# A residual stored before its affine part, and modulation steps spread anew

## The chip, the cores and the metric

The kernel is one program on one core of a Trainium2 chip. The metric is the device time of one execution in microseconds (us). Everything is fp32; TensorE (PE) multiplies each fp32 operand as a high and a low half, so one product of two fp32 tiles is three matrix instructions. VectorE (DVE) and ScalarE (ACT) prepare those halves, SyncE (SP) issues nearly all transfers from one queue, in order, and GpSimd (POOL) does little.

## The reference, cut to what matters

A two-layer backbone works on 512 latent tokens and 256 context tokens of width 1024. Each layer has a half-step SwiGLU feed-forward, a mixer (layer 0: a bidirectional HGRN2 recurrence, layer 1: a chunked spatial-gating MLP), and a second feed-forward. Each of these is wrapped in the same way:

```python
def modulate(x, m, k):
    return x * (1 + m[..., 3 * k + 1, :]) + m[..., 3 * k, :]

def post_norm_update(x, y, m, k, g, b):
    return layer_norm(DN_ALPHA * x + m[..., 3 * k + 2, :] * y, g, b)

def macaron_half_ffn(x, m, k, w_in, w_out, g, b):
    return post_norm_update(x, 0.5 * swiglu(modulate(x, m, k), w_in, w_out), m, k, g, b)

def chunk_mlp(h, n_chunks, w_in, v_g, v_b, w_s, b_s, w_out):
    u, v = jnp.split(jax.nn.gelu(h @ w_in), 2, axis=-1)
    v = layer_norm(v, v_g, v_b)
    v = v.reshape(bsz, n_chunks, CM_CHUNK, CM_GROUPS, CM_INNER // CM_GROUPS)
    v = jnp.einsum('gts,bnsgc->bntgc', w_s, v) + b_s.T[None, None, :, :, None]
    return (u * v.reshape(bsz, length, CM_INNER)) @ w_out

    mx = modulation(c, mod_w[i], mod_b[i])     # silu(c) @ mod_w + mod_b: nine rows of 1024
    x = macaron_half_ffn(x, mx, 0, ...)        # ffn (i, 0), context too where it is needed
    x = post_norm_update(x, mixer(modulate(x, mx, 1)), mx, 1, ...)
    x = macaron_half_ffn(x, mx, 2, ...)        # ffn (i, 1)
```

The residual that goes from one wrapped sub-layer to the next is the layer norm's result, g * z + b, where z is the row less its mean and divided by its deviation. The next sub-layer reads it twice: modulated, as the operand of its first product, and times alpha in its own sum before the norm.

## The kernel before

**Stages.** In order of time: ffn (0,0) of the latent, then of the context (`FeedContext`); the HGRN heads; ffn (0,1); ffn (1,0); the chunk MLP, first its value half (8 groups of 4 token tiles), then its gating half (8 groups `gi` of 3 column tiles `ci`), then its output product; ffn (1,1). A weight tile of 512 KB comes by one transfer into `raw` (3 buffers), is split into its halves by ACT (L136) and DVE (L137), and stands in `w` (6 buffers); this is `unit`, L140.

**A feed-forward** has an up half and a down half. The up half after the first two feature tiles is `FeedSums.rest`: for each of 22 tiles f it loads a gate tile `raw` and an up tile `rawu` and replaces eight block products by seven. DVE makes the sums of weights for it (L572 to L576, on `e`, `rawu`, `raw`) and splits four tiles; PE then does seven products of twelve matrix instructions into `psc`, `pse` and `psa`. The down half is `OutPhase`. `lead` and `part` multiply the hidden tiles `hs` with the weights into `y`; `evac` adds `y` to the residual tile `x` and gathers statistics; `norm` makes z in place (L329); `operand` transposes z on PE into `pt` (L339) and applies norm affine and modulation in one step (L349, L351) to give `xm`.

**The transition** is what stands between the last `y` of one sub-layer and the steady loop of the next. In it PE does transposes and, as `xm` comes in, the first products `psf` of the next sub-layer (`staged`); DVE does `evac`, `norm`, `operand`, and then `FeedSums.sums` (L532), which builds the token sums `f4` to `f7` for the seven products. Right behind these, the residual is stored: `store` (L288 to L299) loads g and b as rows (`rg`, `rb`), makes alpha * (g * z + b) in 16 DVE instructions (L296, L297, 128x512 each) and sends 8 transfers of 256 KB to `x2`, `x3`, `x4` or `x5`. The next `OutPhase` loads those tiles back and adds `y` without more ado (`scaled` is True).

**The modulation rows** come from 18 products of a vector with a 1024x1024 matrix, which DVE does beside the other work. One task of `mod_task` is one such matrix: eight steps, each with a 512 KB transfer into `mraw` (2 buffers) and two DVE instructions per condition (L171, `junk`). `mod_step(n)` takes n steps off the queue; calls stand in the loops of the latent ffn (0,0), of the context (one step per feature tile and per pair of hidden tiles), of the HGRN heads (2 and 5 per head from head 1 on) and of the value half of the chunk MLP (one per token tile). `made` drains the queue up to a row that is needed now.

**The order of the work.** Each engine works its list in order. The list is made by a scheduler that moves instructions within what data and buffers permit; `issue_after` holds an instruction behind another.

## Time and profile before

| | before |
|---|---|
| time, median of 3 runs (lowest to highest) | 2534.65 us (2533.74 to 2537.7) |
| the profiled execution's own time | 2532.92 us |
| its span, from the first to the last instruction | 2531.2 us |
| mean granted TensorE clock in it | 0.992 |
| PE busy, share of the span | 2449.0 us, 97% |
| DVE busy, share of the span | 1882.1 us, 74% |
| ACT busy, share of the span | 1100.1 us, 43% |
| transfers | 368.06 MB, mean 145 GB/s |

The span is 1.7 us shorter than that execution's time, and the median of the runs is another 1.7 us longer. PE is busy nearly all the time, so what counts is where it is not, and where it ran at a lower clock. The stages, on the time axis of the profile: latent ffn (0,0) to about 395 us, the context to 590 us, HGRN heads 680 to 1010 us, ffn (0,1) to 1377 us, ffn (1,0) to 1740 us, value half to 1876 us, gating half to 2020 us, its output product to 2163 us, ffn (1,1) to the end. The transitions are at 1010 to 1067, 1377 to 1418, 1732 to 1762 and 2163 to 2212 us.

### The profile page before, as it was taken

To read this page: it belongs to the slowest core of one execution; us is meant where nothing else is said; L and a number is where in the kernel's file an instruction comes from. 1 tells how busy PE (TensorE), PEld (TensorE's weight loads), DVE (VectorE), ACT (ScalarE), POOL (GpSimd) and SP (SyncE) were. 2 spreads that over 40 slices of the span, in tenths; PEclk is the share of its full clock that TensorE was granted. 3 is DMA by queue.
4 is the path that set the end of the run, shared out by engine and by line. 5 is a ranking of instruction groups with operands and counts; after the bars stand their busy time and mean duration, and the time that the engine had idled before them with its cause. 6 is when DMAs were issued, how large, how long until landed. Compare 5 with 4: busy or idle time off the path is not lost.

```text
span 2531.2 us, 37425 instructions
## 1 busy us (share of the span) xinstructions
PE 2449.0 (97%) x14687; PEld 2199.0 (87%) x14687; DVE 1882.1 (74%) x3361; ACT 1100.1 (43%) x1671; POOL 49.3 (2%) x82
## 2 busy tenths in 40 slices
PE   7999999999999899899999999999999999899998
PEld 5888889978888788899988999988998888899987
DVE  7965479784599986988756988657787345988765
ACT  4222434453444452455643555533332233455641
POOL 0000000000000000000000000000010000000001
PEclk9999999999999999999999999999999999999999
DMA  8866357974234414333332433324963223333332
GB/s 320 290 200 198 104 171 237 313 251 132 69 123 134 142 59 142 121 117 101 126 112 71 167 103 114 110 96 156 312 202 109 83 92 114 114 114 109 109 101 79
DMA packets 111170, 368.06 MB, mean 145 GB/s; under 512 B 12760, under 2 KB 16016, under 8 KB 110992
## 3 DMA queue, kind: packets, MB, share of 16 engines
q1 hardware_dynamic: 110992, 365.65, 43.5%
q8 instruction: 115, 1.88, 0.3%
q14 instruction: 63, 0.52, 0.1%
HBM read 352.99 MB, written 12.61 MB: 144 GB/s over the span
## 4 chain that ended last, share of the span: by engine, by line
PE 69%; DVE 17%; DMA 7%; ACT 3%; issue 2%; POOL 1%; SPq 0%; POOLq 0%; DVEq 0%; ACTq 0%
PE y L151 7%; PE y L149 7%; PE y L150 7%; PE psc L149 4%; PE psc L151 4%; PE psc L150 4%; PE psf L150 4%; PE psf L151 3%; PE psf L149 3%; DVE junk L171 2%; PE pse L149 2%; DVE w L137 2%; PE pse L151 2%; PE pse L150 2%; DMA raw<-in_ffn_w_in 2%
## 5 line engine op out<-in xcount | busy, mean ns | idle before, releaser
L137 DVE TENSOR_TENSOR w<-raw,w 128x1024 fp32r<-128x1024 f32 (+1 forms) x458 | 516.0, 1131 | 181.8 <-ACT w L136 179.6
L136 ACT ACTIVATE w<-raw 128x1024 fp32r<-128x1024 f32 (+1 forms) x458 | 449.7, 984 | 405.7 <-PE y L151 91.2
L149 PE MATMUL y<-w,hs 128*128 128x512 f32 x984 | 384.5, 391 | 4.4 <-ACT hs L136 4.4
L151 PE MATMUL y<-w,hs 128*128 128x512 f32 x984 | 384.6, 391 | 2.3 <-DVE hs L137 2.3
L150 PE MATMUL y<-w,hs 128*128 128x512 f32 x984 | 383.5, 390 | 0.0
L137 DVE TENSOR_TENSOR hs<-h,hs 128x512 fp32r<-128x512 f32 (+1 forms) x220 | 136.1, 635 | 151.0 <-ACT hs L136 151.0
L136 ACT ACTIVATE hs<-h 128x512 fp32r<-128x512 f32 (+1 forms) x220 | 126.2, 587 | 241.1 <-PE y L151 230.9
L151 PEld LDWEIGHTS y<-w,hs 128*128 128x128 f32 x984 | 185.1, 188 | 44.7 <-DVE hs L137 6.1
L149 PEld LDWEIGHTS y<-w,hs 128*128 128x128 f32 x984 | 185.2, 188 | 44.5 <-ACT hs L136 6.6
L150 PEld LDWEIGHTS y<-w,hs 128*128 128x128 f32 x984 | 185.1, 188 | 38.0
L149 PE MATMUL psf<-xm,w 128*128 128x512 f32 (+1 forms) x544 | 192.0, 361 | 19.0 <-ACT xm L136 18.6
L151 PE MATMUL psf<-xm,w 128*128 128x512 f32 (+1 forms) x544 | 193.8, 357 | 1.5 <-DVE w L137 1.5
L150 PE MATMUL psf<-xm,w 128*128 128x512 f32 (+1 forms) x544 | 194.5, 359 | 0.5 <-DVE xm L137 0.5
L171 DVE SCALAR_TENSOR_TENSOR junk<-mraw,srow_x 128x512 bf16<-128x512 f32 x256 | 165.7, 684 | 13.9 <-DMA mraw<-in_mod_w 13.9
L149 PE MATMUL pse<-f,w 128*128 128x256 f32 x480 | 137.2, 286 | 6.9 <-ACT silu L483 6.9
L151 PE MATMUL psc<-xm,w 128*128 128x256 f32 x480 | 136.2, 284 | 4.0 <-DVE w L137 4.0
L150 PE MATMUL pse<-f,w 128*128 128x256 f32 x480 | 136.9, 285 | 0.0
L151 PE MATMUL pse<-f,w 128*128 128x256 f32 x480 | 136.9, 285 | 0.0
L149 PE MATMUL psc<-f,w 128*128 128x256 f32 x480 | 136.5, 284 | 0.0
L150 PE MATMUL psc<-f,w 128*128 128x256 f32 x480 | 136.2, 284 | 0.0
L151 PE MATMUL psc<-f,w 128*128 128x256 f32 x480 | 136.1, 284 | 0.0
L149 PE MATMUL psc<-xm,w 128*128 128x256 f32 x480 | 135.8, 283 | 0.0
(258 smaller groups left out, 5913.2 us busy)
## 6 DMA issues: line engine op xcount, KB each, us to landing
raw<-in_ffn_w_in SPq DMA_DIRECT2D x160, 512.0 KB, 4.5
mraw<-in_mod_w SPq DMA_DIRECT2D x144, 512.0 KB, 4.6
raw<-in_ffn_w_out SPq DMA_DIRECT2D x110, 512.0 KB, 3.6
rawu<-in_ffn_w_in SPq DMA_DIRECT2D x60, 512.0 KB, 3.5
raw<-in_hg_wf SPq DMA_DIRECT2D x32, 512.0 KB, 4.3
raw<-in_cm_wv SPq DMA_DIRECT2D x32, 384.0 KB, 4.5
raw<-in_cm_wu SPq DMA_DIRECT2D x24, 512.0 KB, 3.8
raw<-in_cm_w_out SPq DMA_DIRECT2D x24, 512.0 KB, 3.4
```

What stands on the lines that cost most here:

```text
L136: nc.scalar.activation(dst_hi, src, AF.Copy)
L137: latest[0] = nc.vector.tensor_tensor(dst_lo, src, dst_hi.bitcast(F32), ALU.subtract)
L149: nc.tensor.matmul(ps, ah, bh, start=start, stop=False, **kw)
L150: nc.tensor.matmul(ps, ah, bl, start=False, stop=False, **kw)
L151: return nc.tensor.matmul(ps, al, bh, start=False, stop=stop, **kw)
L171: nc.vector.scalar_tensor_tensor(junk, w[:, c], 1.0, s[:, c], ALU.mult, ALU.mult, dst[:, i : i + 1])
```

## The change

**The residual** x2 to x5 is stored as z: four transfers of 512 KB straight from the tiles that `norm` wrote, with no DVE work. The `OutPhase` that reads it gets `affine`, the index of the norm whose g and b are due; it does three pairs of hidden tiles first (`lead(0, 3)`) and then `finish`, which loads g and b and does the same 16 DVE instructions on the tiles it has loaded. Only x1, written ahead of the context's ffn, is stored as before. **The first weight sums:** in `FeedSums.rest` the operands of the first feature tile are held behind the last instruction of `sums`.

**The modulation steps:** `mod_step` counts in fractions. The context's two loops take half a step each time where they took one, and the tasks for it are queued before the latent loop instead of within it. The HGRN heads take seven steps each from head 0 on, where they took seven from head 1 on in parts of two and five (two after the second forget product, five after the outputs), and the steps of a head now stand behind the `queries` of head 0. The value half of the chunk MLP takes none; the gating half takes two for each `ci`, and closes the queue at its last group.

```diff
-    def mod_step(n):
-        while n > 0 and mod_queue:
+    def mod_step(n, after=None):
+        credit[0] += n
+        while credit[0] >= 1 and mod_queue:
             try:
-                with tc.issue_after(latest[0].ins):
+                with tc.issue_after((after or latest[0]).ins):
                     next(mod_queue[0])
-                n -= 1
+                credit[0] -= 1
...
+        def finish(self):
+            for hf in range(2):
+                c = slice(hf * HC, (hf + 1) * HC)
+                g, b = (load_row(self.bp, tag, src[self.affine][c]) for tag, src in (("rg", ln_g), ("rb", ln_b)))
+                for x in self.xs:
+                    nc.vector.scalar_tensor_tensor(x[:, c], x[:, c], ALPHA, g, ALU.mult, ALU.mult)
+                    nc.vector.scalar_tensor_tensor(x[:, c], b, ALPHA, x[:, c], ALU.mult, ALU.add)
...
+            if self.affine:
+                self.lead(0, 3, nmod)
+                self.finish()
             self.lead(0, self.npair, nmod)
...
             if self.xdst is not None:
-                if nxt.urgent:
-                    with tc.issue_after(last.ins):
-                        for _ in self.store():
-                            pass
+                if nxt.whole:
+                    nxt.later = self.store()
                 else:
-                    nxt.later = self.store()
+                    for t, z in enumerate(self.xs):
+                        nc.sync.dma_start(self.xdst(t), z)
...
+            first = len(self.hs)
+            for f in range(first, NF):
+                if f == first:
+                    with tc.issue_after(self.summed.ins):
+                        wg, we, wu, w4 = operands(f)
+                else:
+                    wg, we, wu, w4 = operands(f)
...
+        for l, ch in ((0, 5), (0, 7), (0, 6), (0, 8), (1, 2)):
+            queue_mod(modp, srow, l, ch, ["x"])
         hget = f0.rest(hp, 2)
...
-                for l, ch in ((0, 5), (0, 7), (0, 6), (0, 8), (1, 2)):
-                    queue_mod(modp, srow, l, ch, ["x"])
...
-            hget = f1.rest(hp, 1)
+            hget = f1.rest(hp, 0.5)
...
-            ).run(bp, None, 1)
+            ).run(bp, None, 0.5)
...
-                mod_step(2 if h else 0)
...
+                    if h == 0:
+                        for ch in (1, 0, 4, 3):
+                            queue_mod(modp, srow, 1, ch, ["x"])
+                        first = ready
...
+                if h < NH:
+                    mod_step(7, first)
                 if prev:
                     on = outputs(h - 1, prev)
-                    mod_step(5)
...
-                    mod_step(1)
                     nc.scalar.activation(vt[:, t, :], ps[:, :GC], AF.Gelu_apprx_tanh)
...
-            for ch in (5, 7, 6, 8):
-                made((1, ch, "x"))
-            early.close()
...
+                if gi == NG - 1:
+                    for ch in (5, 7, 6, 8):
+                        made((1, ch, "x"))
+                    early.close()
                 for ci in range(3):
...
+                    mod_step(2)
                     nc.vector.tensor_tensor(ht[:, ci, :], tb.rearrange("p n t -> p (n t)"), u, ALU.mult)
```

**How the instructions move.** First, DVE at the end of the last transition (into ffn (1,1)), from the last two token sums on (`bw` are the blocks of the transposed operand, `f` the sums split for PE). Before:

```order
L137 TENSOR_TENSOR f_19934<-bw_20014,f_19934 128x512
L296 SCALAR_TENSOR_TENSOR x<-x,rg 128x512 x2
L297 SCALAR_TENSOR_TENSOR x<-rb,x 128x512 x2
L296 SCALAR_TENSOR_TENSOR x<-x,rg 128x512 x2
L297 SCALAR_TENSOR_TENSOR x<-rb,x 128x512 x2
L137 TENSOR_TENSOR w<-rawu,w 128x1024
L137 TENSOR_TENSOR w<-raw,w 128x512
L296 SCALAR_TENSOR_TENSOR x<-x,rg 128x512 x4
L297 SCALAR_TENSOR_TENSOR x<-rb,x 128x512 x4
L137 TENSOR_TENSOR w<-raw,w 128x1024
```

Now:

```order
L137 TENSOR_TENSOR f_19922<-bw_20002,f_19922 128x512
L137 TENSOR_TENSOR w<-raw,w 128x1024
L591 TENSOR_TENSOR e<-raw,rawu 128x512 x2
L592 TENSOR_TENSOR rawu<-rawu 128x512 x2
L593 SCALAR_TENSOR_TENSOR e<-rawu,raw 128x512 x2
L504 TENSOR_TENSOR h<-psf,silu 128x512
L137 TENSOR_TENSOR w<-e,w 128x1024
L595 SCALAR_TENSOR_TENSOR raw<-raw,e 128x512
L504 TENSOR_TENSOR h<-psf,silu 128x512
L137 TENSOR_TENSOR w<-rawu,w 128x1024
```

The 16 instructions of the store are gone from here (they stand in the loop over f that follows), and the weight sums and splits of the first feature tile, which before stood ahead of the token sums, now begin here.

Second, SP's queue in the HGRN heads, where `raw` is a projection's weight tile and `mraw` a modulation step's matrix. Before:

```order
L177 DMA mraw<-in_mod_w 128x1024 x5
L142 DMA raw<-in_hg_wf 128x1024 x3
L177 DMA mraw<-in_mod_w 128x1024 x7
L142 DMA raw<-in_hg_wf 128x1024 x3
L177 DMA mraw<-in_mod_w 128x1024 x7
L142 DMA raw<-in_hg_wf 128x1024 x3
L177 DMA mraw<-in_mod_w 128x1024 x7
L142 DMA raw<-in_hg_wf 128x1024 x5
```

Now:

```order
L177 DMA mraw<-in_mod_w 128x1024 x5
L142 DMA raw<-in_hg_wf 128x1024 x2
L177 DMA mraw<-in_mod_w 128x1024 x3
L142 DMA raw<-in_hg_wf 128x1024
L177 DMA mraw<-in_mod_w 128x1024 x2
L142 DMA raw<-in_hg_wf 128x1024
L177 DMA mraw<-in_mod_w 128x1024 x3
L142 DMA raw<-in_hg_wf 128x1024 x2
L177 DMA mraw<-in_mod_w 128x1024 x3
L142 DMA raw<-in_hg_wf 128x1024
L177 DMA mraw<-in_mod_w 128x1024 x2
L142 DMA raw<-in_hg_wf 128x1024
```

Weights no longer stand behind seven matrices in a row, but between two and three.

Third, DVE in the gating half, one `ci` and part of the next (`tb` and `ht` follow the PE work of a `ci`, `vt` is the value of the next group). Before:

```order
L1166 SCALAR_TENSOR_TENSOR vt<-vt,cmv_17952,gb 128x384
L1188 TENSOR_TENSOR tb<-pscs,bsr 128x512
L137 TENSOR_TENSOR w<-raw,w 128x1024
L1192 TENSOR_TENSOR ht<-tb,u 128x512
L1169 SCALAR_TENSOR_TENSOR vt<-vt,crs_17950,gb 128x384
```

Now:

```order
L1216 TENSOR_TENSOR tb<-pscs,bsr 128x512
L171 SCALAR_TENSOR_TENSOR junk,acc_x<-mraw,srow_x 128x512
L1221 TENSOR_TENSOR ht<-tb,u 128x512
L171 SCALAR_TENSOR_TENSOR junk,acc_x<-mraw,srow_x 128x512 x2
L137 TENSOR_TENSOR w<-raw,w 128x1024 x2
L171 SCALAR_TENSOR_TENSOR junk,acc_x<-mraw,srow_x 128x512 x2
L1216 TENSOR_TENSOR tb<-pscs,bsr 128x512
L171 SCALAR_TENSOR_TENSOR junk,acc_x<-mraw,srow_x 128x512
L1221 TENSOR_TENSOR ht<-tb,u 128x512
```

Four instructions on `mraw` (two steps) stand in each `ci` among the `tb`, `ht` and the splits of the weights.

More of the change, by code (lines that the diff above doesn't have):

```diff
@@ L200, in queue_mod @@
         mod_queue.append(mod_task(modp, srow, l, ch, conds))
-    def mod_step(n):
-        while n > 0 and mod_queue:
+    credit = [0.0]
+    def mod_step(n, after=None):
+        credit[0] += n
+        while credit[0] >= 1 and mod_queue:
             try:
-                with tc.issue_after(latest[0].ins):
+                with tc.issue_after((after or latest[0]).ins):
                     next(mod_queue[0])
-                n -= 1
+                credit[0] -= 1
             except StopIteration:
                 mod_queue.pop(0)
+        if not mod_queue:
+            credit[0] = 0.0
     def made(key):
@@ L214, in made @@
         while key not in d:
-            mod_step(1)
+            mod_step(1 - credit[0])
         return d[key]
@@ L237, in backbone_kernel @@
     class OutPhase:
+        affine = None
         def __init__(self, hget, nk, units, nt, l, j, cond, yscale, xsrc, scaled, after, xm, xdst, nxt, tail=2):
@@ L430, in backbone_kernel @@
     class Phase:
-        urgent, later = True, iter(())
+        whole, later = False, iter(())
         def load(self):
@@ L533, in add @@
                     ks = slice(2 * j, 2 * j + 2)
-                    split(dst[:, 0, ks, :], dst[:, 1, ks, :], a)
+                    self.summed = split(dst[:, 0, ks, :], dst[:, 1, ks, :], a)
             add(self.f4, (0, 0), (1, 0))
@@ L557, in product, with weights, operands @@
                     )
-            for f in range(len(self.hs), NF):
+            def weights(src, n=D):
+                w = wpool.tile([P, 2, D], F32R, tag="w", name="w", bufs=6)
+                split(w[:, 0, :n], w[:, 1, :n], src[:, :n])
+                return w
+            def operands(f):
                 g = wpool.tile([P, D], F32, tag="raw", name="raw", bufs=3)
@@ L564, in rest @@
                 e = sp.tile([P, D], F32, tag="e", name="e", bufs=2)
-                def weights(src, n=D):
-                    w = wpool.tile([P, 2, D], F32R, tag="w", name="w", bufs=6)
-                    split(w[:, 0, :n], w[:, 1, :n], src[:, :n])
-                    return w
                 wg = weights(g)
@@ L577, in rest @@
                 wu = weights(u)
-                w4 = weights(g, K2)
+                return wg, we, wu, weights(g, K2)
+            first = len(self.hs)
[5 more added lines that the diff above has]
+                    wg, we, wu, w4 = operands(f)
                 pc, pe, pa = bank("psc"), bank("pse"), bank("psa")
@@ L613, in backbone_kernel @@
     class FeedContext(FeedIn):
-        urgent = False
+        whole = True
         def ahead(self, i):
@@ L757, in backbone_kernel @@
         srow = {"x": silu_row(modp, "x")}
-        for ch in (1, 0, 4, 3):
-            queue_mod(modp, srow, 1, ch, ["x"])
         def late_outputs():
@@ L897, in queries @@
                 nc.scalar.activation(r.kkn[:, :, r.d, :], r.kk[:, :NT, near], AF.Copy)
-                nc.vector.tensor_tensor(r.Q, r.Q, q.rearrange("p (s t) -> p s t", t=P), ALU.mult)
+                return nc.vector.tensor_tensor(r.Q, r.Q, q.rearrange("p (s t) -> p s t", t=P), ALU.mult)
             def transposed(blocks):
@@ L1038, in backbone_kernel @@
                     for r in (n0, n1):
-                        queries(r, q)
+                        ready = queries(r, q)
+                    if h == 0:
+                        for ch in (1, 0, 4, 3):
+                            queue_mod(modp, srow, 1, ch, ["x"])
+                        first = ready
                 else:
@@ L1072, in backbone_kernel @@
         )
-        op.nhs = 8
+        op.nhs, op.affine = 8, (0, 1)
         op.run(bp)
@@ L1106, in backbone_kernel @@
         )
-        op.nhs = 8
+        op.nhs, op.affine = 8, (0, 2)
         op.run(bp)
@@ L1119, in backbone_kernel @@
         )
-        op.bp = bp
+        op.bp, op.affine = bp, (1, 0)
         early = ExitStack()
@@ L1143, in backbone_kernel @@
                         cm_tok(ps, xm, ws, t)
-                    mod_step(1)
                     nc.scalar.activation(vt[:, t, :], ps[:, :GC], AF.Gelu_apprx_tanh)
                     nc.vector.bn_stats(st[t][:, gi, :], vt[:, t, :])
-            for ch in (5, 7, 6, 8):
-                made((1, ch, "x"))
-            early.close()
             stat = []
@@ L1200, in backbone_kernel @@
         hget = f4.rest(hp, sp)
-        OutPhase(
+        op = OutPhase(
             hget, NF, ffn_units(1, 1), NT, 1, 2, "x", 0.5, lambda t: x5[t], True, None,
             None, lambda t: out[t], None, tail=4,
-        ).run(bp)
+        )
+        op.affine = (1, 1)
+        op.run(bp)
 def _feature_units(w):
```

## The prediction

> **What bounds the kernel now.** I read the page first, then the waits of PE by what released them, then a table of stretches cut at the stages, and last the timeline at the places those two name.

> ```profile
> span 2531.2 us, 37425 instructions
> PE 2449.0 (97%) x14687; PEld 2199.0 (87%) x14687; DVE 1882.1 (74%) x3361; ACT 1100.1 (43%) x1671; POOL 49.3 (2%) x82
> ```

> PE is idle for 2531.2 - 2449.0 = 82.2 us. The change takes no matrix instruction away, so those microseconds, and whatever a lower clock costs, are all that can be won. The waits of PE (in total, how often, the longest) name who was late:

> ```profile
> PE psf L149 <- ACT xm L136: 18.6, 4, 12.6
> PE psfl L151 <- DVE w L137: 7.1, 1, 7.1
> PE pse L149 <- ACT silu L483: 6.9, 2, 3.8
> PE pt L339 <- DVE x L329: 6.3, 4, 4.0
> PE po L981 <- DVE Sc L962: 5.4, 6, 1.5
> PE y L149 <- ACT hs L136: 4.4, 3, 3.9
> PE psc L151 <- DVE w L137: 4.0, 4, 1.5
> PE pto L998 <- DVE on L992: 3.8, 4, 1.3
> PE pscv L149 <- ACT w L136: 2.5, 1, 2.5
> ```

> Nearly all are split operands and normalised rows that DVE and ACT owe to PE; the longest, 12.6, is the start of the program. The table of stretches has width and busy time of PE, PEld, DVE, ACT and POOL, then the granted clock, the DMA share and GB/s:

> ```profile
> 500.00:580.00 80.00, 73.30 (x345) 57.70 (x344) 65.11 (x132) 42.67 (x70) 0.00 (x0) 0.98 0.78 261
> 680.00:920.00 240.00, 221.77 (x1330) 195.32 (x1330) 223.69 (x570) 115.08 (x175) 5.88 (x6) 0.99 0.38 119
> 860.00:900.00 40.00, 32.38 (x196) 28.96 (x196) 36.44 (x85) 18.69 (x29) 1.01 (x1) 0.91 0.37 119
> 1010.00:1070.00 60.00, 49.45 (x364) 47.20 (x364) 55.06 (x90) 28.72 (x45) 4.19 (x8) 0.91 0.37 121
> 1370.00:1420.00 50.00, 45.59 (x342) 43.66 (x341) 45.43 (x75) 24.88 (x40) 3.24 (x6) 0.97 0.27 89
> 1725.00:1800.00 75.00, 67.77 (x387) 64.61 (x386) 62.00 (x129) 29.16 (x46) 2.98 (x6) 1.00 0.67 231
> 2155.00:2215.00 60.00, 52.09 (x377) 49.99 (x376) 54.71 (x88) 28.68 (x45) 3.62 (x6) 0.91 0.33 115
> ```

> Idle PE, as width less busy: context output 6.7, heads 18.2 (7.6 of it in 860 to 900), the four transitions 10.6, 4.4, 7.2 and 7.9: 55 us of the 82; the rest is start and end, which the change leaves alone. Beside it PE lost work at a lower clock, (1 - clock) times the width: 1.6, 3.6, 5.4, 1.5, 0 and 5.4, in all 17.5 us. So 72.5 us is the ceiling. The clock falls right behind idle time, as the last transition shows: a wait of 2.60 us, and then a stretch at half:

> ```profile
> 2166.20 1.00 PE L149 MATMUL psf<-xm,w 128*128 128x256 f32 x4 [2.60 <-ACT xm L136]
> 2166.50:2169.90 3.40, 3.40 (x17) 3.17 (x16) 3.34 (x8) 1.56 (x3) 0.30 (x2) 0.50 0.00 0
> ```

> A stretch of 3.4 us at half costs 1.7 us of work, and one of double length 3.4; a wait of 2.6 or more is thus worth more than its own length.

> **The residual and the first weight sums, at the transitions.** In the transition at 1010 the end of DVE's token sums, the store, and the next weights read so:

> ```profile
> 1044.91 1.28 DVE L296 SCALAR_TENSOR_TENSOR x<-x,rg 128x512 f32<-128x512 f32 x2
> 1052.99 2.50 DVE L296 SCALAR_TENSOR_TENSOR x<-x,rg 128x512 f32<-128x512 f32 x4 [0.85 <-DMA rg<-in_ln_g]
> 1056.20 2.50 DVE L297 SCALAR_TENSOR_TENSOR x<-rb,x 128x512 f32<-128x512 f32 x4 [0.71 <-DMA rb<-in_ln_b]
> 1058.61 1.22 DVE L137 TENSOR_TENSOR w<-raw,w 128x1024 fp32r<-128x1024 f32 x1
> 1061.56 1.22 DVE L137 TENSOR_TENSOR w<-e,w 128x1024 fp32r<-128x1024 f32 x1
> 1048.18 0.28 PE L149 MATMUL psc<-xm,w 128*128 128x256 f32 x1
> ```

> Sixteen instructions at 0.60 to 0.63 us (four start to end in 2.50) and 0.85 + 0.71 of waiting for rows keep DVE for some 11 us, and the splits for the second feature tile come at 1058.61 and 1061.56, when PE wants them at about 1058 and 1061. This is where the 6.9 us of `pse` and the 4.0 of `psc` come from; `silu` stands on ACT behind the copies of those same weights. The two `pse` waits are in the transitions at 1010 and 2155, whose clock is 0.91. Each transition also has a stretch behind an earlier gap (`pt`, 4.0, or `psf`, 2.6), of the clock loss 3.4 and 1.7, which leaves 5.4 - 3.4 = 2.0 and 5.4 - 1.7 = 3.7 behind `pse`; I count 5.1 for the two. With the store gone these go: 6.9 + 4.0 + 5.1 = 16.0 us.

> In its place comes a chain that was not there. The weight sums of the first feature tile begin only now at the end of the token sums: one split (1.14 from start to start), the sums of two tiles (six at 0.60), one hidden tile (0.60) and the split of `e` (1.14), in all 6.5 us from 1044.9, to 1051.4. PE reaches `psc` at 1048.18 and has 12 matrix instructions at 0.12 us, 1.4 us, and by its own new order some eleven of `psa` and two of `pse`, 1.5 us, before it needs that split: 1051.1. The rest is about 0.3 us here; the token sums themselves end 0 to 0.6 us earlier since no weight work stands among them. I take 1.3 us in each of three transitions, since ACT's copy and one buffer hand-over come in between, 3.9 in all; bounds 0 (PE just covers it) and 3.3 with a stretch at half (5.0, the price of the longest `pse` wait).

> Holding the weight sums back also shortens `evac` and `norm` at 1010, where two or three of them stand between the first tiles; of the 6.3 us of `pt` I take 2.0, bounds 1 and 6 (with its clock stretch). The first `psf` waits of the other two (3.2 and 2.6) hang on `norm` and `operand` alone: nothing. **Transitions into ffn (0,1), (1,0), (1,1): -16.0 + 3.9 - 2.0 = -14 us, bounds -4 and -22.**

> [...]

> The 16 instructions are not saved but moved, into the loop over f of the reader. A feature tile is 7 x 12 matrix instructions at 0.12 = 10.1 us of PE; two more DVE instructions in each, 1.2 us, fit while DVE is 74% busy. In the chunk MLP they fall in the value half, freed of steps. What `finish` could wait for is the tile it reads, which goes out and comes back:

> ```profile
> x<-x SPq DMA_DIRECT2D x40, 256.0 KB, 3.3
> ...
> 1012.29 0.81 DVE L329 TENSOR_SCALAR x<-x,mv,rstd 128x1024 f32<-128x1024 f32 x1 [0.78 <-POOL rstd L319]
> ...
> 1030.37 0.54 DVE L351 TENSOR_SCALAR bw<-pt,opc 128x256 f32<-128x256 f32 x1
> ```

> At 3.3 to 6.6 us each way (256 KB, and twice that) it is back 7 to 13 us after `norm`. The earliest such instruction stands behind the fifth `bw`, which came 18 us after that `norm`, some 15 without the weight work in between. Covered; if it were not, DVE would hold `xm` and the sums behind it.

> **The value half.** In 1725 to 1800 DVE had the store, 16 instructions, and the steps, and SP the matrices ahead of `cm_wv` weights. PE's idle 7.2 us are one wait for `xm` at the join (1.6, stays) and waits for late weights (`pscv` 2.5 the largest). Both causes leave: **-5.6 us, bounds -4 and -7.**

> **The gating half** takes the steps.

> ```profile
> L137 DVE TENSOR_TENSOR w<-raw,w 128x1024 fp32r<-128x1024 f32 x44 | 53.8, 1222 | 9.5 <-ACT w L136 8.9
> L1188 DVE TENSOR_TENSOR tb<-pscs,bsr 128x512 f32<-128x512 f32 x23 | 15.8, 688 | 54.0 <-PE pscs L1183 54.0
> L1166 DVE SCALAR_TENSOR_TENSOR vt<-vt,cmv,gb 128x384 f32<-128x384 f32 x24 | 13.7, 605 | 0.9 <-DMA gb<-in_cm_v_g 0.9
> 1890.00:2020.00 130.00, 130.00 (x659) 110.69 (x658) 79.16 (x116) 35.66 (x47) 0.00 (x0) 1.00 0.32 101
> 1800.00:1876.00 76.00, 76.00 (x441) 76.00 (x440) 54.36 (x130) 25.17 (x37) 3.35 (x5) 1.00 0.79 267
> mraw<-in_mod_w SPq DMA_DIRECT2D x144, 512.0 KB, 4.6
> ```

> A `ci` takes PE about 130 / 22 = 5.9 us, with no idle time. DVE needs, from start to start, 1.14 for `w`, 0.6 + 0.6 for `tb` and `ht`, 8/3 x 0.53 = 1.4 for `vt` (0.08 less than its busy time, as four of 0.68 overlapped to 2.50 above), and now 2.5 for two steps (four instructions): 6.2 us. So DVE falls behind by 0.3 us in each of 16 `ci`, 5 us, against a lead of about two weight tiles. Transfers are 1.57 MB per `ci`, 267 GB/s, which the value half moved with PE full. A slot of `mraw` turns round in 4.6 + 1.2 = 5.8. All three limits lie within 0.3 us of PE's 5.9. **+1 us, bounds 0 and +6.**

> **The context.** Half the steps take 1.25 us of DVE in every second pair and a quarter of a pair's transfers away. In 500 to 580 all but about 1.5 us of 6.7 idle and 1.6 at lower clock hang on late `w` and `hs`: **-6.8 us, bounds -4 and -9.** The steps go to the latent output loop before it, where the first row shows nothing against them.

> **The heads.**

> ```profile
> 840.51 26.59 SPq L177 DMA_DIRECT2D mraw<-in_mod_w  x7
> 873.40 6.10 SPq L142 DMA_DIRECT2D raw<-in_hg_wf  x4
> 873.39 0.80 PE L151 MATMUL psfl<-xm,w 128*128 128x512 f32 x1 [7.10 <-DVE w L137]
> ```

> Seven matrices in a row hold SP's queue for 26.6 us and the weights wait behind them; by the fourth such head the lead is used up, and PE stands 7.1 us plus 3.6 at half clock. With two or three between weights that goes, unless DVE, full in these heads, hands the splits over late; I take 7 of the 10.7. `po` and `pto`, 9.2 us in all, are steps in DVE's way; head 0 has room and takes seven, but the other heads keep theirs: 0. **-7 us, bounds 0 and -13.**

> **Sum:** -14 - 5.6 + 1 - 6.8 - 7 = -32.4; 2532.92 - 32.4 = 2500.5 for the profiled execution, and 1.7 more for the median: 2502.2 us.

> **The rivals.**

> *The new chain is as long as the old wait.* If the split of `e` comes 3.3 us late in each of three transitions, each with a stretch at half, they cost 15.0 in place of 3.9: 2513. For it: PE waits in order, DVE is 54 to 55 of 60 us busy there. Against it: the sum above, to within 1 us. Chance 0.17.

> *The heads stay as they are,* as DVE bounds them (223.69 of 240 busy): 2509. For it: every step is still done. Against: the 7.1 us wait is one event, behind a queue. Chance 0.08.

> *The change does not do what it says:* `finish` waits for store and reload in front of `xm`, and the 14 us of the transitions come back with some of the rest, 2520 to 2535. Against it: 15 us of work lie ahead of it. Chance 0.06.

> *The gating half becomes the bound (slower).* One mechanism: two `mraw` buffers, three loads per `ci` in one queue. If landing takes 7.2 us in place of 4.6, the slot turns in 8.5, and 16 x (8.5 - 5.9) = 42, less a lead of 12, plus 1.7 at half clock behind each gap of 2.6 (27), is 57 us: about 2559. It decides from a period near 8. For it: nothing stood on DVE's spare time there before. Against: 267 GB/s was carried with PE full. Chance 0.08.

> **How the numbers follow.** The forecast has 0.61. Its own range is 2492 to 2511. The range of 8 in 10 takes in the first two rivals and what lies just above the third's near end: 2488 to 2521. A difference of 0.2%, 5 us, is about what a measurement can tell. Faster: forecast and the first two rivals, 0.86; same 0.05 from the third; slower 0.09, the fourth and the third's far end.

> **What would show it.** Right: no `pse` wait on `silu` over 1.5 us; no wait of 7 us in the heads and at most five matrices in a row; PE full from 1800 through the gating half; clock 0.5 only behind the first `psf` waits. Wrong: `tb` or `vt` among the releasers of PE in the gating half, `mraw` as what DVE waits for there, or a new wait of `pse` on DVE's `w` at the head of the loop over f.

## The result, and the profile after

| | before | changed |
|---|---|---|
| time, median (lowest to highest), 4 runs each side by side | 2536.18 us (2533.74 to 2539.75) | 2500.76 us (2497.92 to 2501.94) |
| ratio to before | | 0.9858, 95% interval 0.9841 to 0.9875 |
| span of the profiled execution | 2531.2 us | 2499.4 us |
| mean granted clock | 0.992 | 0.995 |

The changed kernel's median is 35.4 us below that of the kernel before, which took 1.5 us more here than in the runs that the forecast started from; 2502 was predicted. The spans of the two profiles differ by 31.8 us, so the other 3.6 us of the medians are in no profile. In one of e6's four executions below the granted clock was 0.557 and the time 4050.58 us; no ratio counts it. The head of the changed kernel's page, PE's idle time now being 2499.4 - 2441.6 = 57.8 us against 82.2:

```profile
span 2499.4 us, 37382 instructions
PE 2441.6 (98%) x14687; PEld 2197.6 (88%) x14687; DVE 1880.8 (75%) x3361; ACT 1101.4 (44%) x1671; POOL 47.3 (2%) x82
```

DVE does the same work (1880.8 against 1882.1 us); only its place is another. The waits of PE, in total, how often, and the longest:

```profile
PE psf L149 <- ACT xm L136: 17.9, 4, 12.5
PE pto L1022 <- DVE on L1016: 9.3, 4, 4.2
PE pse L149 <- ACT w L136: 4.1, 3, 2.3
PE po L1005 <- DVE Sc L986: 3.8, 5, 2.3
PE po L1004 <- DVE Sc L986: 3.5, 3, 1.5
PE pt L356 <- DVE x L346: 3.3, 3, 2.8
PE pscv L149 <- ACT xm L136: 1.6, 1, 1.6
PE psf L151 <- DVE w L137: 1.4, 2, 1.0
```

Gone are `pse` on `silu` (6.9), `psc` on `w` (4.0), `psfl` on `w` (7.1), `pscv` on `w` (2.5) and most of `y` on `hs` (4.4). New are `pse` on `w` (1.42, 2.27 and 0.43, one in each transition, 4.1 in all) and a larger `pto` (9.3 against 3.8) in the heads. The stretches of the changed kernel that answer to those shown of before (width, busy PE, PEld, DVE, ACT, POOL, clock, DMA share, GB/s):

```profile
500.00:570.00 70.00, 68.72 (x341) 57.42 (x340) 60.08 (x115) 40.00 (x66) 0.00 (x0) 1.00 0.80 267
640.00:680.00 40.00, 39.50 (x225) 34.62 (x224) 29.95 (x61) 19.95 (x28) 0.00 (x0) 1.00 0.39 127
680.00:720.00 40.00, 32.77 (x183) 28.95 (x182) 39.11 (x106) 19.00 (x28) 1.92 (x1) 0.90 0.51 159
720.00:760.00 40.00, 36.66 (x211) 32.02 (x210) 37.89 (x104) 17.03 (x26) 1.02 (x1) 0.97 0.48 155
1000.00:1060.00 60.00, 53.49 (x409) 51.43 (x409) 55.34 (x90) 32.21 (x51) 3.51 (x8) 0.97 0.34 119
1360.00:1410.00 50.00, 45.87 (x361) 44.79 (x360) 46.97 (x75) 26.93 (x45) 2.52 (x4) 0.97 0.36 122
1715.00:1790.00 75.00, 73.13 (x429) 71.88 (x429) 46.01 (x72) 32.24 (x51) 1.57 (x4) 1.00 0.57 187
1855.00:2005.00 150.00, 149.96 (x755) 127.27 (x754) 128.28 (x261) 40.36 (x55) 1.80 (x3) 1.00 0.63 200
2135.00:2190.00 55.00, 52.72 (x420) 51.12 (x420) 51.18 (x81) 33.04 (x53) 2.52 (x4) 1.00 0.38 130
```

The gating half (1855 to 2005) has taken the steps, DVE 128 of 150 us busy, and PE is still full. Only the heads look worse.

To see what each part gave, I cut both traces at the same places of the program, namely where PE begins a new kind of product, and took the differences. These times are worked out from the start of the first matrix instruction of each kind:

| stretch of the program | before | changed | difference | forecast |
|---|---|---|---|---|
| latent and context ffn, from the first `y` to the first `psv` | 322.7 | 312.3 | -10.4 | -6.8 |
| values, to the first `psfl` | 67.1 | 67.2 | +0.1 | 0 |
| heads, to the first `y` of their output | 299.5 | 302.2 | +2.7 | -7 |
| head output and transition, to the first `psc` | 98.8 | 96.4 | -2.3 | |
| loop over f of ffn (0,1), to its first `y` | 207.7 | 203.5 | -4.2 | |
| its down half and transition | 151.3 | 148.6 | -2.7 | |
| loop over f of ffn (1,0) | 203.6 | 205.7 | +2.1 | |
| chunk MLP's output and transition | 162.5 | 160.4 | -2.1 | |
| loop over f of ffn (1,1) | 209.3 | 202.6 | -6.8 | |
| *the six of the transitions together* | | | *-16.0* | *-14* |
| value half, `pscv` to `pscu` | 142.3 | 135.9 | -6.4 | -5.6 |
| gating half, to the first `y` | 153.9 | 152.1 | -1.8 | +1 |
| all | | | -31.8 | -32.4 |

Profiles of the same code differ in such stretches: with the changed context the first was 312.1 to 315.9 us, and a value half with no steps 135.6 to 137.2. The sum came out, but three of its terms did not: the heads, the context, and, as the runs below show, what stands inside the -16.0.

### The profile page after: what moved, and what is told of

Read it like the earlier page. It is cut to its first block, busy times and chain, and to the rows that moved or that the text cites. A ratio compares the mean times of both kernels' runs of the same rounds, so it can differ in the third digit from the quotient of the medians.

```text
span 2499.4 us, 37382 instructions
## 1 busy us (share of the span) xinstructions
PE 2441.6 (98%) x14687; PEld 2197.6 (88%) x14687; DVE 1880.8 (75%) x3361; ACT 1101.4 (44%) x1671; POOL 47.3 (2%) x82
## 4 chain that ended last, share of the span: by engine, by line
PE 81%; DVE 13%; ACT 2%; DMA 2%; issue 1%; POOL 1%; SPq 0%; POOLq 0%; DVEq 0%; ACTq 0%
PE y L151 8%; PE y L150 8%; PE y L149 8%; PE psf L151 5%; PE psf L150 5%; PE psf L149 5%; PE psc L149 5%; PE psc L151 5%; PE psc L150 5%; PE pse L149 2%; PE pse L151 2%; PE pse L150 2%; PE pscu L149 2%; PE pscu L150 2%; PE pscu L151 2%; PE pscv L151 2%
## 5 line engine op out<-in xcount | busy, mean ns | idle before, releaser
L137 DVE TENSOR_TENSOR w<-raw,w 128x1024 fp32r<-128x1024 f32 (+1 forms) x458 | 516.5, 1132 | 167.5 <-ACT w L136 165.7
L136 ACT ACTIVATE w<-raw 128x1024 fp32r<-128x1024 f32 (+1 forms) x458 | 449.7, 984 | 431.4 <-PE y L151 83.2
L151 PE MATMUL y<-w,hs 128*128 128x512 f32 x984 | 383.1, 389 | 0.8 <-DVE hs L137 0.8
L149 PE MATMUL y<-w,hs 128*128 128x512 f32 x984 | 383.2, 389 | 0.5 <-ACT hs L136 0.5
L137 DVE TENSOR_TENSOR hs<-h,hs 128x512 fp32r<-128x512 f32 (+1 forms) x220 | 136.3, 636 | 143.7 <-ACT hs L136 143.6
L136 ACT ACTIVATE hs<-h 128x512 fp32r<-128x512 f32 (+1 forms) x220 | 127.2, 588 | 251.5 <-PE y L151 241.5
L151 PEld LDWEIGHTS y<-w,hs 128*128 128x128 f32 x984 | 184.7, 188 | 40.0 <-DVE hs L137 1.8
L149 PEld LDWEIGHTS y<-w,hs 128*128 128x128 f32 x984 | 184.7, 188 | 39.4 <-ACT hs L136 0.9
L149 PE MATMUL psf<-xm,w 128*128 128x512 f32 (+1 forms) x544 | 191.8, 359 | 18.5 <-ACT xm L136 17.9
L151 PE MATMUL psf<-xm,w 128*128 128x512 f32 (+1 forms) x544 | 193.0, 356 | 1.4 <-DVE w L137 1.4
L149 PE MATMUL pse<-f,w 128*128 128x256 f32 x480 | 136.5, 284 | 4.1 <-ACT w L136 4.1
L151 PE MATMUL pse<-f,w 128*128 128x256 f32 x480 | 136.4, 284 | 0.0
L149 PE MATMUL psc<-f,w 128*128 128x256 f32 x480 | 136.1, 284 | 0.0
L149 PE MATMUL psc<-xm,w 128*128 128x256 f32 x480 | 135.8, 283 | 0.0
L150 PE MATMUL psc<-xm,w 128*128 128x256 f32 x480 | 135.8, 283 | 0.0
L151 PE MATMUL psc<-xm,w 128*128 128x256 f32 x480 | 135.8, 283 | 0.0
L151 PE MATMUL psc<-f,w 128*128 128x256 f32 x480 | 135.8, 283 | 0.0
## 6 DMA issues: line engine op xcount, KB each, us to landing
raw<-in_ffn_w_in SPq DMA_DIRECT2D x160, 512.0 KB, 4.5
mraw<-in_mod_w SPq DMA_DIRECT2D x144, 512.0 KB, 4.5
raw<-in_ffn_w_out SPq DMA_DIRECT2D x110, 512.0 KB, 3.6
rawu<-in_ffn_w_in SPq DMA_DIRECT2D x60, 512.0 KB, 3.5
x<-x SPq DMA_DIRECT2D x36, 512.0 KB, 3.7
raw<-in_hg_wf SPq DMA_DIRECT2D x32, 512.0 KB, 3.9
raw<-in_cm_wu SPq DMA_DIRECT2D x24, 512.0 KB, 4.4
```

Of the source, the lines that this page charges most:

```text
L136: nc.scalar.activation(dst_hi, src, AF.Copy)
L137: latest[0] = nc.vector.tensor_tensor(dst_lo, src, dst_hi.bitcast(F32), ALU.subtract)
L149: nc.tensor.matmul(ps, ah, bh, start=start, stop=False, **kw)
L150: nc.tensor.matmul(ps, ah, bl, start=False, stop=False, **kw)
L151: return nc.tensor.matmul(ps, al, bh, start=False, stop=stop, **kw)
```

## The experiments

All times are medians of four runs (ten for e2), each beside the kernel before on the same chip (2532 to 2536 us there). My theory after the result: the moved store gave the gain at the transitions, the hold on the first weight sums is a trade, the heads gained nothing since their steps pile up in head 1, and the context gained by a lower rate of steps.

### Heads as before (e1)

```diff
-                    mod_step(7, first)      # and the tasks queued in head 0
+                mod_step(2 if h else 0)     # behind the second forget product
+                    mod_step(5)             # behind the outputs
```

> The changed kernel with the heads' steps as before (2 and 5 per head from head 1 on); all else as changed. In the changed kernel the stretch from the first psfl to the first y of the HGRN output is 302.2 us, before 299.5. Theory A (the steps of heads 0 and 1 pile up in head 1, DVE full there): the stretch is 299.5 again, with one psfl wait of about 7 us in the fourth head with steps; 2498 us. Rival (the new waits come from what stands ahead of the heads, the context's steps): pto and po waits of head 1 stay, the stretch stays at 302, 2501 us. Rival 2 (the old psfl wait was a consequence of the context's loads and is gone by itself): the stretch is near 289, 2490 us.

2499.92 us, 0.9859 of before (0.9844 to 0.9874): no difference to the changed kernel. The heads took 300.2 us, and the old wait stood in the list again, in place of the large `pto`:

```profile
PE psfl L151 <- DVE w L137: 7.1, 1, 7.1
PE po L1007 <- DVE Sc L988: 5.7, 6, 1.7
PE pto L1024 <- DVE on L1018: 3.8, 4, 1.3
```

So the heads' part of the change takes one wait away and makes others of the same size. Seven profiles of heads with the new order (the changed kernel and e2 to e6 and e10) gave 300.1 to 303.2 us, two with the old one 299.5 and 300.2: no gain, perhaps a loss of a microsecond or two. The queue of the changed kernel shows why:

```profile
676.46 0.33 SPq L142 DMA_DIRECT2D raw<-in_hg_wf  x1
678.15 31.71 SPq L177 DMA_DIRECT2D mraw<-in_mod_w  x8
710.72 0.33 SPq L142 DMA_DIRECT2D raw<-in_hg_wf  x1
```

The list of the new order, as shown with the change, begins behind these eight. The steps may not start before the `queries` of head 0, which is near that head's end, so the seven of head 0 and those of head 1 come together: eight matrices in a row, and DVE busy 39.1 of 40 us from 680 to 720. PE then waited 4.2 us for `on`, which is behind them on DVE.

### The store back (e2), and store back with no hold (e6)

```diff
-                    for t, z in enumerate(self.xs):
-                        nc.sync.dma_start(self.xdst(t), z)
+                    with tc.issue_after(last.ins):
+                        for _ in self.store():
+                            pass
```

In both, `affine` is left out too; e6 also takes the hold on the first weight sums away.

> The changed kernel with the residual stored with its affine part behind the sums, as before; the hold on the first weight sums stays. Theory (the store is what held PE in the transitions): the waits of pse and psc come back, 10 to 16 us, 2511 to 2517 us. Rival (the hold on the weight sums is what helped): within 3 us of the changed kernel's 2501.

> The changed kernel without both the hold and the moved store: transitions as before, only the steps as changed. Theory (the store alone cost some 16 us, the hold is no gain by itself): the three loops over f take 207.7, 203.6 and 209.3 again from the first psc to the first y, against 201.6 each without hold and store; 2516 us. Rival (hold and store need each other): 2505 us or less.

e2: 2532.98 us, 0.9992 of before (0.9983 to 1.0002). With the store back but the hold kept, the whole gain is gone: 32 us, where 10 to 16 were expected. e6: 2518.28 us, 0.9937 (0.9920 to 0.9955). The loops over f:

| | ffn (0,1) | ffn (1,0) | ffn (1,1) |
|---|---|---|---|
| before | 207.7 | 203.6 | 209.3 |
| changed | 203.5 | 205.7 | 202.6 |
| e2, store and hold | 213.2 | 215.9 | 212.8 |
| e6, store, no hold | 207.5 | 203.8 | 210.1 |
| e3, no store, no hold | 201.6 | 201.6 | 201.6 |

e6 has the transitions of before (17 us over the changed kernel), so they owe their gain to store and hold alone. Between e6 and e3 only the store differs: 6 + 2 + 8.5 = 16.5 us in these loops. In e2 DVE has the store and the weight chain one after another, and the weight sums of the first feature tile begin only at 1410.91, behind nearly all of the store, where in the changed kernel they follow the sums at once:

```profile
1403.52 1.21 DVE L137 TENSOR_TENSOR w<-raw,w 128x1024 fp32r<-128x1024 f32 x1
1404.66 0.68 DVE L505 TENSOR_TENSOR h<-psf,silu 128x512 f32<-128x512 f32 x1
1406.04 1.90 DVE L304 SCALAR_TENSOR_TENSOR x<-x,rg 128x512 f32<-128x512 f32 x3 [0.70 <-DMA rg<-in_ln_g]
1408.49 1.90 DVE L305 SCALAR_TENSOR_TENSOR x<-rb,x 128x512 f32<-128x512 f32 x3 [0.56 <-DMA rb<-in_ln_b]
...
1410.91 0.68 DVE L592 TENSOR_TENSOR e<-raw,rawu 128x512 f32<-128x512 f32 x1
...
1415.12 1.22 DVE L137 TENSOR_TENSOR w<-e,w 128x1024 fp32r<-128x1024 f32 x1
```

PE's waits of `pse` on `w` add up to 25.1 us in e2, 8.9 the longest.

### No hold (e3)

```diff
-                if f == first:
-                    with tc.issue_after(self.summed.ins):
-                        wg, we, wu, w4 = operands(f)
-                else:
-                    wg, we, wu, w4 = operands(f)
+                wg, we, wu, w4 = operands(f)
```

> The changed kernel without the hold on the first weight sums, so that these may stand ahead of the token sums again; the store stays gone. Theory (the hold is a trade: it shortens the pt wait at 1004 by 1 to 2 us and costs the 4.1 us of the new pse waits): 2498 to 2503 us, pse waits on ACT's w gone, pt waits up. Rival (the hold carries a good part of the transitions' gain): 2506 us or more.

2501.25 us, 0.9864 (0.9849 to 0.9878): the same as the changed kernel. The three loops over f are 7.0 us shorter in all (201.6 each), and the three stretches ahead of them 4.4 us longer (97.2, 149.9 and 162.7 against 96.4, 148.6 and 160.4). In the five profiles that have this hold and the moved store (the changed kernel, e1, e4, e5 and e10) the loops are 4.8 to 7.1 us longer in all than in e3. The wait of `pse` on `w` is not in the list, and `pt` is back:

```profile
PE pt L356 <- DVE x L346: 5.0, 3, 3.9
```

The hold is a trade, then. What it costs is seen in the changed kernel, in the transition at 1363 to 1395, from the end of the token sums on:

```profile
1386.99 0.68 DVE L137 TENSOR_TENSOR f<-h,f 128x512 fp32r<-128x512 f32 x1
1387.59 1.22 DVE L137 TENSOR_TENSOR w<-raw,w 128x1024 fp32r<-128x1024 f32 x1
1388.73 1.28 DVE L591 TENSOR_TENSOR e<-raw,rawu 128x512 f32<-128x512 f32 x2
...
1390.54 1.28 DVE L592 TENSOR_TENSOR rawu<-rawu 128x512 f32<-128x512 f32 x2
...
1392.34 1.28 DVE L593 SCALAR_TENSOR_TENSOR e<-rawu,raw 128x512 f32<-128x512 f32 x2
1394.14 1.22 DVE L137 TENSOR_TENSOR w<-e,w 128x1024 fp32r<-128x1024 f32 x1
```

and on ACT and PE at the same place, where `psc` began at 1390.29:

```profile
1393.05 1.06 ACT L136 ACTIVATE w<-e 128x1024 fp32r<-128x1024 f32 x1 [0.74 <-DVE e L593]
1394.16 0.39 PE L149 MATMUL pse<-f,w 128*128 128x256 f32 x1 [2.27 <-ACT w L136]
```

PE went on when ACT's half of the split of `e` was done, at 1394.11; DVE's half only begins then.

### The value half's steps back (e4)

```diff
+                    mod_step(1)             # per token tile of the value half
...
-                    mod_step(2)             # per ci of the gating half
```

> The changed kernel with the chunk MLP's steps back in the value half, one per token tile. Theory (the steps made the weights late there): the value half takes 6 us more, 2507 us. Rival (the store at the join made them late, and it is gone): 2501 us, value half as now, 135.9 us.

The queue is also closed ahead of the gating half again. 2512.01 us, 0.9903 (0.9888 to 0.9917). The runs are 11 us above the changed kernel. The profiled execution was the fastest of them (2506.72 us); in it the value half took 139.8 us (+4.0) and the gating half 153.0 (+1.0), with late weights (`pscv` on `w` 2.5) and `vt` (1.2) in the list of waits. So the steps made the weights late, and the store at the join seems to have made it worse only where they were: the value half took 142.3 us with both (before), 139.8 with the steps alone (e4), and 135.7 and 135.6 with the store alone (e2, e6). The first two are one profile each. The other 6 us of the runs' difference are not in that profile, where the context's stretch was 3.6 us longer (315.9) with the same code; where they were in the slower executions stays open.

### The context as before (e5), and only its rate as before (e10)

```diff
-        for l, ch in ((0, 5), (0, 7), (0, 6), (0, 8), (1, 2)):
-            queue_mod(modp, srow, l, ch, ["x"])   # e5: back in the latent output loop; e10: stays
...
-            hget = f1.rest(hp, 0.5)
+            hget = f1.rest(hp, 1)
...
-            ).run(bp, None, 0.5)
+            ).run(bp, None, 1)
```

> The changed kernel with the context's steps as before: a whole step at each place, and the tasks queued within the latent output loop. Theory (steps and weights share one queue and one memory there, so the rate of the steps sets how late the weights are): the stretch from the first y of the latent to the first psv is 322 again, against 312 to 316; 2510 us. Rival (the gain there is the smaller number of steps in the context alone, because nine steps moved ahead): a stretch between 315 and 320, the wait of y on hs of 4 us back only in part; 2505 us.

> The changed kernel with a whole step at each place in the context's two loops, the tasks still queued ahead of the latent loop. Theory (the rate of the steps sets how late the weights are): stretch from the first y of the latent to the first psv near 319, as with both parts undone, 2507 us. Rival (nine steps fewer in the context are what helped): 312 to 315, 2501 us.

e5: 2507.97 us, 0.9897 (0.9879 to 0.9916), and a stretch of 319.9 us; of the wait of `y` on `hs` 2.0 us came back. e10: 2499.74 us, 0.9859 (0.9844 to 0.9874), and 314.3 us. The rival holds: with the tasks queued ahead, a whole step at each place costs nothing that these runs can tell. Counted in the traces, the context's loops (395 to 590) held 30 steps before, 21 in the changed kernel and 21 in e10; the others had moved into the latent output loop. Their rate does not matter: e10 does 20 of its 21 before 510 us and the changed kernel 11. What counts is how many there are in the context in all.

```profile
510.00:580.00 70.00, 68.15 (x308) 56.02 (x307) 56.22 (x89) 42.46 (x68) 1.85 (x2) 1.00 0.67 208
```

This is e10 in that loop; before, PE was busy 63.3 of the same 70 us, with the clock at 0.98.

### Steps of the heads, spread and moved (e7, e8)

Both have no hold, as e3, and are to be compared with it (2501.25 us, heads 300.1).

```diff
-                    mod_step(7, first)
+                    mod_step(16 / 3, first)       # e7: 32 steps over six heads
+                    mod_step(8 / 3, first)        # e8: 16 steps over six heads
...
-            for l, ch in ((0, 8), (1, 2)):        # e8: two rows more, ahead of the heads
-                made((l, ch, "x"))
+            for ch in (1, 0):
+                queue_mod(modp, srow, 1, ch, ["x"])
+            for l, ch in ((0, 8), (1, 2), (1, 1), (1, 0)):
+                made((l, ch, "x"))
...
-                        for ch in (1, 0, 4, 3):
+                        for ch in (4, 3):     # e8: what is left for the heads
```

> The changed kernel without the hold, and with the 32 steps spread evenly over heads 0 to 5 (five or six each) in place of seven in heads 0 to 3 and four in head 4. Theory (a head has room for about five steps: 37.4 us a head without steps, DVE 33 of them): the stretch from the first psfl to the first y falls from 300 to about 291; 2491 us. Rival (steps begin only behind the queries of head 0, so those of heads 0 and 1 still meet in head 1): 296 to 298, 2496 us, with pto and po waits in head 1 only.

> The changed kernel without the hold, and with two of the four rows (16 steps) taken ahead of the heads, while the HGRN values are multiplied; the other 16 are spread over heads 0 to 5. Theory (the heads lose because DVE is full; in 580 to 640 it is not): heads near 284, values stretch 67 as now; 2484 us. Rival (the queue: matrices ahead of the heads' first weights make these late): values and first heads take 5 to 10 us more; 2490 us or above.

e7: 2496.55 us, 0.9854 (0.9839 to 0.9869), heads 297.2: the rival's range, with `pto` still 3.5 at its longest, in head 1. e8: 2489.59 us, 0.9826 (0.9811 to 0.9841), heads 291.3, values 67.2 as always. The theory's direction holds, not its size: 284 was expected. A wait of 2.7 us of `ptk` appeared at the first head, and the granted clock was 0.92 from 640 to 680 us. DVE took the 16 steps ahead of the heads without a wait on PE:

```profile
570.00:640.00 70.00, 70.00 (x319) 58.05 (x319) 43.13 (x112) 16.32 (x24) 5.64 (x12) 1.00 0.63 203
```

### The hold moved to the last norm (e9)

```diff
-            nc.vector.tensor_scalar(z, z, mv[:, 0:1], rstd, ALU.subtract, ALU.mult)
+            self.nxt.normed = nc.vector.tensor_scalar(z, z, mv[:, 0:1], rstd, ALU.subtract, ALU.mult)
...
-                if f == first:
-                    with tc.issue_after(self.summed.ins):
+                if f < first + 2:
+                    with tc.issue_after(self.normed.ins):
```

with the heads of e8. The hold now covers the first two feature tiles, where it covered one.

> The changed kernel with the heads' steps as in the run with half of them ahead, and with the first weight sums held behind the last norm of a transition in place of behind the last token sum. Theory (the hold gains by keeping weight work out of evac and norm, and loses by the chain behind the token sums): the loops over f stay at 201.6 each, and the stretches up to the first psc are those of the changed kernel (96.4, 148.6, 160.4) or within 1 us of them, against 98.0, 151.7 and 162.3 with no hold; 2483 to 2486 us. Rival (DVE is full in the transition, and whatever stands ahead of the token sums makes these late): the loops over f lose 1 to 3 us each; 2488 us or above.

2483.50 us, 0.9792 of before (0.9776 to 0.9809): the fastest kernel of this study, 17 us under the changed one. The loops over f are 201.6 each and the stretches ahead of them 95.4, 150.1 and 160.4, where e8 had 98.0, 151.7 and 162.3: the hold's gain (in the middle one 1.5 us less of it than the changed kernel) and not its cost. What the place and the second tile give singly was not run. In the list of waits neither `pse` nor a `pt` above 1.7 us is left:

```profile
PE pkl L984 <- ACT kT L932: 4.6, 3, 1.8
PE po L1007 <- DVE Sc L988: 2.8, 6, 0.8
PE pt L356 <- DVE x L346: 2.2, 3, 1.7
```

### More steps ahead of the heads (e11, e12)

```diff
-            for ch in (1, 0):
+            for ch in (1, 0, 4):            # e11; (1, 0, 4, 3) in e12
...
```

The rest is e9, with the 8 steps left in e11 spread over heads 0 to 5 and none left in e12.

> As the run with the hold behind the last norm, but three of the four rows (24 steps) ahead of the heads and one (8 steps) in heads 0 to 5. Theory (the heads lose what DVE cannot do within 37.4 us a head; ahead of them DVE is free for more): heads 291 to about 286, 2478 us. Rival (the space ahead is full with 16 steps, and more of them run into heads 0 and 1, with waits of ptk and pssn there): heads 291 or more, 2483 us or above.

> As before, with all four rows (32 steps) ahead of the heads. Theory: no step is left after head 1; heads 283 if the 67 us of the values hold all 32 steps (39 us of DVE beside 26), 2476 us. Rival (DVE or the transfers, some 17 MB in 67 us, are full): values and head 0 together lose what the later heads win; 2483 us or above.

e11: 2502.73 us, 0.9877 (0.9861 to 0.9894); e12: 2518.35 us, 0.9949 (0.9932 to 0.9965). The rivals hold. The `ptk` wait that e11's rival named came (6.1 us in e11, 6.3 in e12), but the longest wait, 11.0 us in e11 and 31.86 in e12, has a mechanism that I had not named. PE and ACT in e12:

```profile
677.75 0.58 PE L149 MATMUL psfc<-xmc,w 128*128 128x256 f32 x1 [31.86 <-ACT v L843]
```

```profile
677.10 1.57 ACT L843 ACTIVATE v<-psv 128x512 f32<-128x512 f32 x3 [60.88 <-DVE junk L171]
```

The values `v` of the heads share no data with the steps, but the program gives them memory that the steps use until their end, so the last values wait for the last `junk`, and PE for the PSUM banks that they free. In e9 the same instruction also waited (to 637.57 us, for `junk`), but PE did not. More steps in the queue are not done faster beside the values: between 572 and 640 us all of e9's last 18 were done, and no more than 19.5 in e11 and 19 in e12, one in about 3.6 us, with DVE waiting 17.9 us for `mraw` in e12. From 641 to 673 us, when PE waited nearly all the time, e12 did one in 2.5 us. Sixteen fit; 24 do not.

## Why the prediction was right, and where it was not

The time, 2502.2 by the sum, was 2500.76. By its steps:

- **The store at the transitions: -16.0 forecast.** Confirmed: the loops over f fall by 15.8 us from before to e3, and by 16.5 from e6 to e3, and in e3 PE has no wait of `pse` or `psc` left. The stretches ahead of them, for which I had no term, fell by 2.7 more in e3, no more than some of them differ between profiles (the middle one 149.9 in e3, 151.7 in e8).
- **The new chain: +3.9 forecast.** It costs 7.0 (changed against e3; 4.8 to 7.1 over five profiles). The failing step is the cover. The sum counted "some eleven of `psa`" among what PE does "before it needs that split". In the changed kernel two of `pse` (1394.16) and two of `psc` (1394.50) come ahead of `psa` (1394.73), and PE took them in that order, so `psa` covered nothing. The chain's length was right (6.5 us forecast, 6.6 from 1387.59 to 1394.16), though not its links: it holds two hidden tiles, not one, and ends with ACT's half of the split, not DVE's. The rival that had this chain 3.3 us late in all three transitions, each with a stretch at half clock, was right that PE waits in each, but the longest wait is 2.27 us, and only that one is followed by half clock.
- **`evac` and `norm` freed: -2.0, at 1010 only.** It is -4.4 in the three stretches. The forecast "nothing" for the other two failed: their first `psf` waits fell from 3.2 and 2.6 us to 1.8 each, so they did not hang on `norm` and `operand` alone.
- **`finish`:** no wait on the reloaded tile. PE's list has none, and the loops of e3 and e9, with `finish` in them, are at 201.6 in all three ffns. In the changed kernel four of its 16 instructions still stand in the first transition ahead of the last token sum, and five in the second, one of them (1386.39) right ahead of that sum.
- **Value half: -5.6, measured -6.4.** The steps are the cause; the store, which I named beside them, costs 2.4 on top of them, by one profile each, and nothing without them.
- **Gating half: +1, measured -1.8.** No `ci` is lost; the wait on `vt` at its entrance (2.1 us before) is gone. Why, no run isolates. The rival of a gating half bound by `mraw` is out.
- **Context: -6.8, measured -10.4 (7 by e5's time, 10 by its ratio).** The mechanism was wrong: I gave the gain to the half rate. e10 shows that the eight or nine steps moved ahead give it; the forecast took these only as harmless.
- **Heads: -7, measured +2.7 (0 within what profiles of the same code differ).** The wait of 7.1 us did go as forecast. Its price was read too high: of the 6.83 us at half clock 3.96 lay inside the wait itself, so it cost 7.1 + 1.4 = 8.5 us and not 10.7. (Counted so, half clock cost 12.6 us in all before, and the ceiling was 67.6, not 72.5.) The failing step is "head 0 has room and takes seven": the room of head 0 ends before its `queries`, behind which the steps are held. They run in head 1, DVE is full there (39.1 of the 40 us from 680 to 720), and the rival "the heads stay as they are" had the right reason. "At most five matrices in a row" failed at the same place, with eight.

Of the signs, `pse` on `silu` is gone, no wait in the heads is longer than 4.2 us, and PE is full through the gating half (149.96 of 150 us). But the half clock came also in the heads (at 705, 716 and 760, behind PE's waits of 2.32, 4.18 and 3.38 us) and behind the `pse` wait at 1394, and the sign of being wrong, a new wait of `pse` at the head of the loop over f, is there, on ACT's `w` in place of DVE's.

The errors in the heads (+9.7) and in the context (-3.6), and those of the chain (+3.1), `norm` (-2.4), gating half (-2.8) and the rest nearly cancel. So the total was right partly by luck.

## What to carry to other kernels

When an instruction is taken out of a critical stretch, write down what stands behind it in the list of the engine that waits, in order: here `psa` (1394.73), behind `pse` (1394.16) in PE's list, covered nothing. Here a hold served better at the point where the work it protects ends (the last norm) than at the end of the stretch. To move side work into an idle stretch, look where the first instruction of it may start and where the last must end, including whose memory it keeps, before counting free time.

## What was not expected of the hardware

In the traces of both kernels the stretches of the clock lie on a grid. By the clock records of its trace, the half clock of the changed kernel begins at 705.30, 715.54, 759.91, 1012.50 and 1394.79 us; the distances, 10.24, 44.37, 252.59 and 382.29 us, are 3, 13, 74 and 112 times 3.413 us, and each stretch is 3.413 or 6.827 us long. In e12's long wait the clock was 0.50 through all the 30 us from 651 to 681. The length of a wait does not tell by itself whether the half clock follows: in the changed kernel a wait of 2.27 us at 1394 was followed by it and one of 1.83 at 2142 not. In e9 one of 1.84 was, and in e3 one of 3.18 was not. First the changed kernel, then e9, then e3:

```profile
1394.80:1398.20 3.40, 3.40 (x18) 3.40 (x18) 3.40 (x5) 2.67 (x4) 0.00 (x0) 0.50 0.14 25
2142.00:2146.00 4.00, 3.57 (x27) 3.33 (x28) 3.41 (x8) 2.64 (x5) 0.79 (x2) 1.00 0.18 72
```

```profile
1351.17 0.74 PE L149 MATMUL psf<-xm,w 128*128 128x256 f32 x4 [1.84 <-ACT xm L136]
1352.20:1355.40 3.20, 3.20 (x15) 3.20 (x16) 2.61 (x6) 1.24 (x3) 0.79 (x2) 0.50 0.82 286
```

```profile
1364.31 0.73 PE L149 MATMUL psf<-xm,w 128*128 128x256 f32 x4 [3.18 <-ACT xm L136]
1364.31:1367.71 3.40, 3.37 (x26) 3.13 (x27) 2.81 (x7) 2.23 (x4) 0.79 (x2) 1.00 0.89 282
```

```profile
1774.84 0.44 PE L149 MATMUL pscv<-w,xm 128*128 128x384 f32 x1 [2.54 <-ACT w L136]
1770.55:1773.96 3.41, 1.74 (x11) 1.42 (x9) 2.39 (x7) 0.51 (x2) 0.00 (x0) 1.00 0.94 353
1773.96:1777.37 3.41, 1.91 (x9) 1.65 (x10) 2.76 (x6) 1.67 (x2) 0.00 (x0) 1.00 0.76 243
1777.37:1780.78 3.41, 2.14 (x14) 1.80 (x12) 2.75 (x9) 0.84 (x1) 0.00 (x0) 1.00 0.96 318
```

The prediction's bound, a wait of 2.6 us, was too high for e9, where 1.84 us was enough, and too low for e3, where 3.18 was not.
